# A hybrid encoder block on one core: when raw weight tiles are loaded and summed, and where the sine tables stand

## The chip, the cores and the metric

The kernel runs on one core of one Trainium2 chip. The time is device microseconds of one execution; of several executions the median is given. The core has five engines that run their own instruction streams: the matmul engine (PE), two that work on vectors (DVE and ACT), POOL, and SP, which here only issues DMAs. Each engine takes its instructions in the order in which they were put into its stream; between engines they wait for each other by semaphores.

## The reference

One layer on 512 tokens of width 1024, in float32: a SwiGLU FFN (inner width 2816) at half weight, a mixer of gated DeltaNet heads beside multi-head latent attention, and a second FFN. Each part reads a modulated norm of the stream.

```
mod = sc @ w_ada[l] + b_ada[l]
sh1, s1, g1, sh2, s2, g2, sh3, s3, g3 = jnp.split(mod, N_MOD, axis=-1)
h = _modulate(x, sh1, s1)
x = x + 0.5 * g1[:, None, :] * _swiglu(h, ffn1_w_in[l], ffn1_w_out[l])
h = _modulate(x, sh2, s2)
y = _hybrid_mixer(h, cos, sin, w_in[l], ...)
x = x + g2[:, None, :] * y
h = _modulate(x, sh3, s3)
x = x + 0.5 * g3[:, None, :] * _swiglu(h, ffn2_w_in[l], ffn2_w_out[l])
```

`cos` and `sin` are taken of the positions times 32 frequencies; the attention's rotary keys and queries use them. `mod` is the product of the 1024 conditioning values with a 1024 x 9216 matrix.

## The kernel before

**Products in three parts.** Every float32 product runs as three matmuls (`mm3`, lines 278 to 282, and 906 to 908 for the pairs): a high part of the weight (`wh`, a rounded copy made by ACT) and of the activation, and the low parts that are left (`wl`, the difference, made by DVE). A raw weight tile (`wr`, 512 KB, four buffers) is loaded by SP, copied to its high part by ACT, and subtracted to its low part by DVE.

**FFN1** (`ffn1`, `ffn_pairs`) runs as a hand-written order: one counter of steps, and for every step a list of tasks (`add(step, task)`); `tick` runs the tasks of a step, then come the step's matmuls, then `side.step`. Within `in_order` every engine keeps the order in which the instructions are written. Steps 0 to 47 are the units of inner columns 6 to 11 (8 steps each, `whole` and `piece`); their SwiGLU activation is `glu_steps`, at the end of the unit. From step 48 (`begin`) ten pairs follow, one for each of the inner column blocks 12 to 21, 7 steps apart (`base` = 48, 55, ..., 111; `stop` = 111). Beside them the down projection is fed at 1 to 1.33 products a step (`down`, whose weights are loaded 8 steps ahead of their use, `add(s - 8)`).

**A pair** (`pair_tasks`, `product`) is one gate column block and one up column block, computed with seven products of half width instead of eight. It takes two raw tiles, `g` and `u`. Its tasks, as steps from its base: `load` (-11, both tiles, on SP); `sums` (-7, lines 802 and 803, DVE: `sx` and `sy` from `g` and `u`), `sums2` (-5, DVE); the high part of `u` (-6, line 825, ACT); its low part, which here is not a subtraction on DVE: ACT writes the negated high tile (-5, line 836) and an accumulating DMA on POOL's queue adds the raw tile to it (`add_low`, -4, line 843); high and low parts of `x` (-4, -3) and `y` (-3, -2); of the second half of `g` (0, 1). Then, while PE runs the products `up0` (0), `up1` (1), `s2` (3), `s3` (4), `s1` (6), `s4` (9), `gate1` (12), the accumulator is copied between them by ACT (`early_copy`, line 849: `cc` at 1, `uc` at 4, `cc` again at 7), and the activation is put together: `both` (8), `gate1` (9), `act1` (11), `gate0` (13, lines 858 and 859), `act0` (15, lines 868 and 870: the product `cc` and its high part `ah`), `act_low` (16, line 874: `al`). `s2` adds to the accumulator that `early_copy` at 1 reads, so PE's `s2` waits for that copy.

**The side work** (`Side`, `side.step(n)`: resume a generator n times) holds first the modulation sums (`ada`): 112 tiles of `w_ada`, each loaded by POOL's queue (line 579) and added with a scale on DVE (line 590), one a resumption. It takes 121 resumptions, 81 of them done by step 48. Behind it stands `mixer_consts`: its first resumption issues the loads of the small vectors (`cw`, `vb`, positions) on SP, the fifth transposes `cw` on PE (line 1187) and copies `cwT` and the positions on DVE (lines 1189, 1191), the sixth transposes the positions (line 1194) and forms the angles; then come the sine and cosine by range reduction and polynomials (`sincos`, lines 1269 to 1307) and the rotary tables (lines 1217, 1219): 53 DVE operations. In the pairs' stage `side.step` runs in 3 of 7 steps for the first three pairs and 5 of 7 after, one resumption each; from step 111, two a step.

**Behind the pairs** (steps 111 to 123 and `close`) the last 6 blocks of the down projection run (`units`: high part line 1052, low part line 1056), while the last pair is finished. Then the norm of the mixer follows in two halves (lines 454 to 482), and `latents`: the first projections (three units with both halves of the tokens), a fourth, and so on; `gather` splits them. `mixer` then runs dense units of four parts each with side chains beside them (`dense_units`, `Rates`); the rotary tables are first read in `prep_q`. Outside `in_order` the instructions of an engine can be put into another order than that of the program.

Of the kernel before, what the change touches and what calls it, by code (L numbers as in the profile page):

```python
# [18 lines left out]
P = 128  # L19
# [70 lines left out]
class Block:  # L90
# [687 lines left out]
        yield  # L778
        v.tensor_tensor(out=fl, in0=t, in1=fh.bitcast(F32), op=ALU.subtract)

    def pair_tasks(self, w, f, base, add, room=None, side=None):


        nc, v = self.nc, self.nc.vector
        r = {}
        late = 1 if side else 0
        flat = lambda t: t.rearrange("p k f -> p (k f)")
        A, B = slice(0, NT), slice(NT, 2 * NT)

# [38 lines left out]
        def lo(name, src, part=slice(0, 2 * NT)):  # L828
            def go():
                if name == "g1" and room:  # L830
                    for i in range(2):
                        v.tensor_tensor(out=r["g1l"][i], in0=r[src][:, part.start + i * HALF:part.start + i * HALF + HALF],
                                        in1=r["g1h"][i].bitcast(F32), op=ALU.subtract)
                    return
                if name == "u" and side:
                    nc.scalar.activation(r["ul"], r["u"], AF.Copy, scale=-1.0)
                    return
                v.tensor_tensor(out=r[name + "l"], in0=r[src][:, part], in1=r[name + "h"].bitcast(F32), op=ALU.subtract)
            return go

        def add_low():
            if side:
                nc.gpsimd.dma_start(r["ul"].bitcast(F32), r["u"], accum_op=ALU.add)

        def early_copy(name, part):
            def go():
# [30 lines left out]
        r["do"] = dict(load=load, sums=sums, sums2=sums2)  # L877
        for n, src, part in (("u", "u", slice(0, 2 * NT)), ("x", "x", slice(0, 2 * NT)), ("y", "y", slice(0, 2 * NT)), ("g1", "g", B)):
            r["do"][n] = hi(n, src, part), lo(n, src, part)
        for i, (at, go) in enumerate(((-11, load), (-7, sums), (-5, sums2), (-6, hi("u", "u")), (-5 if side else -4, lo("u", "u")), (-4, hi("x", "x")),  # L880
                       (-3, lo("x", "x")), (-3, hi("y", "y")), (-2, lo("y", "y")), (-1 + late, hi("g1", "g", B)),
                       (0 + late, lo("g1", "g", B)), (1, early_copy("cc", L)), (4, early_copy("uc", L)), (7, early_copy("cc", H)),
                       (8, both), (9, gate1), (11, act1), (13, gate0), (15, act0), (16, act_low), (-4, add_low))):
            by_hand = 11 if base == 0 else 1 if base == 7 else 0
            if i >= by_hand:
                add(base + at, go)
# [47 lines left out]
    def ffn_pairs(self, w1, w2, gate, plain, raws, split, accs, side=None):  # L934
# [7 lines left out]
        begin = 8 * len(grid)  # L942
        base = [begin + 7 * j for j in range(n)]
        stop = base[-1]
        pairs = [self.pair_tasks(w1, plain + j, base[j], add, (2 * (j % 2), 2 * (j % 2) + 1) if side else None, side)
                 for j in range(n)]

        def whole(g, f):

            def load(i):  # L950
                raws[i] = self.raw_unit(w1, i)

            for e in range(2):
                i, s, r = 2 * f + e, 8 * g + 4 * e, {}
                add(s - 9, lambda i=i: load(i))
                add(s - 4, lambda i=i, r=r: next(r.setdefault("g", self.unit_split(raws, split, i))))
                add(s - 3, lambda r=r: next(r["g"], None))
            r = {}
            add(8 * g + 8, lambda: next(r.setdefault("g", self.glu_steps(accs, f))))
            add(8 * g + 9, lambda: next(r["g"], None))  # L960

        def piece(g, f, o):
            i, k = 2 * f + o // 4, 2 * (o % 4)
# [106 lines left out]
        for s in range(0, stop + 13):  # L1070
            if s == begin - 7 and side:
                self.early_pool.__exit__(None, None, None)
                sums = self.tc.tile_pool(name="ws", bufs=1)
                self.ws = sums.__enter__()
            tick(s)
            if s < begin:
                piece(s // 8, grid[s // 8], s % 8)
            for j in range(n):
                if s - base[j] in STEPS:
                    self.product(pairs[j], STEPS[s - base[j]])  # L1080
            for go in fill.pop(s, []):
                go()
            if s in last:
                steps_of(*last[s])
            if side:
                at = s - begin
                side.step(1 + (s % 4 == 0) if at < 0 else at % 7 in ((1, 3, 6) if at < 21 else (0, 1, 3, 4, 6)) if s < stop else 2)
        assert not fill
        if side:
            sums.__exit__(None, None, None)  # L1090
# [73 lines left out]
    def mixer_consts(self):  # L1164
        nc, ins = self.nc, self.ins
        cw = self.slot(s="cw")[:57, :P]
        pos_i = self.slot(I32, s="posi")[:NB, :P]
        vb = self.const([P, 136], s="vb")
        with self.tc.issue_after(self.loaded.ins):
            self.load(cw[:48, :], ins["gdn_conv_w"][0].rearrange("j (t p) -> (j t) p", p=P))  # L1170
            self.load(pos_i, ins["positions"].rearrange("o (b p) -> (o b) p", p=P))
            row = 48
            self.vcol = {}
            for name, n in (("mla_q_norm_w", 3), ("mla_kv_norm_w", 2), ("gdn_norm_w", 1), ("qkn_q_nope", 1),
                            ("qkn_k_nope", 1), ("mla_out_norm_w", 1)):
                self.load(cw[row:row + n, :], ins[name].rearrange("o (t p) -> (o t) p", p=P))
                self.vcol[name] = row
                row += n
            o = 0
            for name, n in (("gdn_a_log", 4), ("gdn_dt_bias", 4), ("qkn_q_rope", 64), ("qkn_k_rope", 64)):  # L1180
                self.load(vb[:, o:o + n], ins[name][0].partition_broadcast(P))
                o += n
        self.alog, self.dtb, self.gqr, self.gkr = vb[:, 0:4], vb[:, 4:8], vb[:, 8:72], vb[:, 72:136]
        for _ in range(4):
            yield
        p = self.aux()
        nc.tensor.transpose(p[:, :57], cw, self.ident[:57, :57])
        self.cwT = self.const([P, 57], s="cwT")
        nc.vector.tensor_copy(self.cwT, p[:, :57])
        pos_f = self.slot(s="posf")[:NB, :P]  # L1190
        nc.vector.tensor_copy(pos_f, pos_i)
        yield
        p = self.aux()
        nc.tensor.transpose(p[:, :NB], pos_f, self.ident[:NB, :NB])
        pos = self.const([P, NB], s="pos")
        nc.vector.tensor_copy(pos, p[:, :NB])


        fr = self.slot(s="fr")[:, :32]
        for i in range(32):  # L1200
            nc.gpsimd.memset(fr[:, i:i + 1], float(np.float32(10000.0 ** (-i / 32.0))))
        ang = self.slot(s="ang")[:, :P]
        av = ang.rearrange("p (b i) -> p b i", b=NB)
        nc.vector.tensor_tensor(out=av, in0=self.bc(pos, NB, 32), in1=fr.unsqueeze(1).to_broadcast([P, NB, 32]),
                                op=ALU.mult)
        yield
        cos, sin = yield from self.sincos(ang)
        yield
        cv, sv = cos.rearrange("p (b i) -> p b i", b=NB), sin.rearrange("p (b i) -> p b i", b=NB)
        self.rope_c, self.rope_s = {}, {}  # L1210
        for nm, gain, sc in (("q", self.gqr, 192.0 ** -0.5), ("k", self.gkr, 1.0)):
            both = self.slot(s="rope").rearrange("p (e b c) -> p e b c", e=2, b=NB)
            c, s = both[:, 0], both[:, 1]
            for j in range(2):
                gj = gain[:, 32 * j:32 * j + 32].unsqueeze(1).to_broadcast([P, NB, 32])
                go = gain[:, 32 - 32 * j:64 - 32 * j].unsqueeze(1).to_broadcast([P, NB, 32])
                nc.vector.scalar_tensor_tensor(out=c[:, :, 32 * j:32 * j + 32], in0=cv, scalar=sc, in1=gj, op0=ALU.mult,
                                               op1=ALU.mult)
                nc.vector.scalar_tensor_tensor(out=s[:, :, 32 * j:32 * j + 32], in0=sv, scalar=sc if j else -sc, in1=go,
                                               op0=ALU.mult, op1=ALU.mult)  # L1220
                yield
            self.rope_c[nm], self.rope_s[nm] = c, s
        self.gqn = self.const([P, 1], s="gqn")
        j = self.vcol["qkn_q_nope"]
        nc.vector.tensor_scalar(out=self.gqn, in0=self.cwT[:, j:j + 1], scalar1=192.0 ** -0.5, scalar2=None, op0=ALU.mult)

    def masks(self):
        nc = self.nc
# [101 lines left out]
    def latents(self, nb):  # L1330
# [8 lines left out]
        def gather(ps):  # L1339
# [8 lines left out]
                    nc.vector.tensor_tensor(out=acc, in0=acc, in1=sq, op=ALU.add)  # L1348
            return parts, acc

        pk = self.proj(self.aux())
        qp, acc = gather(ps)
        ps = [pk]
        lq = qp, self.rms_cols(self.colsum(acc), NB, 384)
        p = self.proj()
# [1 line left out]
        nc.scalar.copy(s[:72, :], p[:72, :])  # L1357
        wq = next(wq)
        ps.append(self.proj())
        kp, acc = gather(ps)  # L1360
        lkv = kp, self.rms_cols(self.colsum(acc), NB, 256)
        wkv = next(wkv)
# [690 lines left out]
    def mixer(self, nb):  # L2053
# [39 lines left out]

        att.add(prepared())

        self.dense_units(4, Rates(sides, (1, 0, 0.25)), 1, conv_done(4, kT))
        chain.flush()
        silu(kT)

# [145 lines left out]
```

## Time and profile before

| what | us |
|---|---|
| median of 3 executions | 1052.04 (1050.21 to 1052.23) |
| the profiled execution | 1052.18 |
| its span, first to last instruction | 1050.2 |
| PE busy in the span | 1022.4 |
| DVE busy | 755.4 |
| ACT busy | 483.2 |

The granted clock of PE is 0.999 of full speed over the span. In the rows of the profile, a line such as "0.9 <-ACT ah L870" behind the last bar says that the engine sat idle for 0.9 us until ACT's instruction of line 870, which writes `ah`, was done. Rows of the timeline give the start, the duration, engine, line, operation, output and inputs, and in brackets the idle time ahead and who ended it. The time of a PE row overlaps with the next one, since matmuls are pipelined: the distance between starts is what one costs. The stretches' rows give, for PE, weight loads, DVE, ACT and POOL, the busy time and the number of instructions.

### The profile page before, as it was taken

The page shows a single profiled execution, that of the slowest core. Times are in us where ns is not written, and L with a number is a line of the kernel's source. Part 1 is how long each engine was busy: PE and PEld are TensorE (multiplying, and loading weights), DVE is VectorE, ACT ScalarE, POOL GpSimd, SP SyncE. Part 2 cuts the span into 40 slices and gives each one's busy share as a digit, 9 for nine tenths or more (in the row PEclk, how much of TensorE's full clock was granted, in tenths as well). Part 3 has the DMA queues.
Part 4 walks back from the last instruction along what each step waited for, and adds up shares of the span by engine and source line. Part 5 has one row for each costly group of instructions (what it writes and reads, how often), then busy time and mean ns, then how long its engine had stood idle before and what let it go on. Part 6 is the DMA issues. An engine that isn't in the chain of part 4 may idle for free. (4 is left out here: it accounts for less than half of the span.)

```text
span 1050.2 us, 17055 instructions
## 1 busy us (share of the span) xinstructions
PE 1022.4 (97%) x6655; PEld 888.4 (85%) x6655; DVE 755.4 (72%) x1414; ACT 483.2 (46%) x864; POOL 114.6 (11%) x232
## 2 busy tenths in 40 slices
PE   7999999999999999999999999999999999999998
PEld 5787878879888979888877768898999999999987
DVE  4477998787788687547976756689768778777642
ACT  4342232255354336649566563465345444444431
POOL 0033331222120101000001011210000000000000
PEclk9999999999999999999999999999999999999999
DMA  9997886676775337611311201073423333333222
GB/s 273 289 272 230 286 245 196 204 193 188 213 200 156 95 96 198 160 41 42 90 51 36 71 22 55 28 161 101 135 78 103 108 101 111 94 98 104 77 61 81
DMA packets 187278, 140.21 MB, mean 134 GB/s; under 512 B 14385, under 2 KB 176190, under 8 KB 187198
## 3 DMA queue, kind: packets, MB, share of 16 engines
q1 hardware_dynamic: 175646, 100.33, 33.4%
q0 software_dynamic: 11552, 38.81, 13.5%
q8 instruction: 52, 0.85, 0.3%
q14 instruction: 28, 0.23, 0.1%
HBM read 127.18 MB, written 2.49 MB: 123 GB/s over the span
## 5 line engine op out<-in xcount | busy, mean ns | idle before, releaser
L280 PE MATMUL pa<-ah,wh 128*128 128x512 f32 (+1 forms) x346 | 133.1, 385 | 1.3 <-ACT ah L870 0.9
L281 PE MATMUL pa<-al,wh 128*128 128x512 f32 (+1 forms) x346 | 132.7, 384 | 1.5 <-DVE al L874 1.5
L282 PE MATMUL pa<-ah,wl 128*128 128x512 f32 (+1 forms) x346 | 131.0, 379 | 0.0
L281 PE MATMUL pa<-hl,wh 128*128 128x512 f32 (+1 forms) x293 | 109.4, 373 | 1.6 <-DVE hl L474 1.4
L280 PE MATMUL pa<-hh,wh 128*128 128x512 f32 (+1 forms) x293 | 110.2, 376 | 0.4 <-ACT hh L482 0.4
L282 PE MATMUL pa<-hh,wl 128*128 128x512 f32 (+1 forms) x293 | 108.5, 370 | 0.0
L579 POOL DMA_DIRECT2D ar<-in_w_ada x112 | 62.9, 606 | 170.1 <-DVE aa L590 63.7
L982 DVE SCALAR_TENSOR_TENSOR xT<-pa,mod,xT 128x512 f32<-128x512 f32 (+1 forms) x79 | 57.3, 728 | 33.1 <-PE pa L282 33.0
L282 PEld LDWEIGHTS pa<-ah,wl 128*128 128x128 f32 x346 | 65.2, 188 | 13.0 <-DVE wl L1056 0.2
L590 DVE SCALAR_TENSOR_TENSOR aa<-ar,sc,aa 128x512 f32<-128x512 f32 x98 | 73.3, 748 | 1.3
L280 PEld LDWEIGHTS pa<-ah,wh 128*128 128x128 f32 x346 | 65.9, 190 | 7.8 <-ACT ah L870 1.3
L281 PEld LDWEIGHTS pa<-al,wh 128*128 128x128 f32 x346 | 65.9, 190 | 7.4 <-DVE al L874 2.2
L906 PE MATMUL pb<-fh,wh 128*128 128x256 f32 x224 | 63.9, 285 | 3.4 <-ACT cc L849 3.3
L280 PEld LDWEIGHTS pa<-hh,wh 128*128 128x128 f32 x293 | 55.3, 189 | 12.4 <-issue 2.9
L281 PEld LDWEIGHTS pa<-hl,wh 128*128 128x128 f32 x293 | 55.3, 189 | 10.5 <-DVE hl L474 2.6
L908 PE MATMUL pb<-hh,wl 128*128 128x256 f32 x224 | 63.4, 283 | 0.7 <-DMA wl<-wr 0.7
L208 DVE TENSOR_TENSOR wl<-wr,wh 128x1024 fp32r<-128x1024 f32 (+1 forms) x33 | 38.5, 1166 | 35.6 <-ACT wh L203 35.4
L282 PEld LDWEIGHTS pa<-hh,wl 128*128 128x128 f32 x293 | 55.3, 189 | 10.3 <-issue 1.2
L908 PE MATMUL pb<-fh,wl 128*128 128x256 f32 x224 | 63.3, 283 | 0.0
L907 PE MATMUL pb<-fl,wh 128*128 128x256 f32 x224 | 63.3, 283 | 0.0
L907 PE MATMUL pb<-hl,wh 128*128 128x256 f32 x224 | 63.3, 282 | 0.0
L906 PE MATMUL pb<-hh,wh 128*128 128x256 f32 x224 | 63.2, 282 | 0.0
(448 smaller groups left out, 2786.9 us busy)
## 6 DMA issues: line engine op xcount, KB each, us to landing
wr<-in_ffn_w_in SPq DMA_DIRECT2D x82, 512.0 KB, 4.0
ar<-in_w_ada POOLq DMA_DIRECT2D x112, 256.0 KB, 4.7
wr<-in_ffn_w_out SPq DMA_DIRECT2D x32, 512.0 KB, 4.0
wr<-in_w_in SPq DMA_DIRECT2D x21, 512.0 KB, 4.1
wl<-wr POOLq DMA_DIRECT2D x18, 512.0 KB, 5.9
ar<-in_w_ada SPq DMA_DIRECT2D x16, 512.0 KB, 8.2
wr<-in_ffn_w_out SPq DMA_DIRECT2D x16, 384.0 KB, 3.6
wr<-in_w_out SPq DMA_DIRECT2D x8, 512.0 KB, 3.4
```

Source lines behind the costliest of these rows:

```text
L208: self.nc.vector.tensor_tensor(out=lo, in0=raw, in1=hi.bitcast(F32), op=ALU.subtract)
L280: mm(out, wh, xh, start=start, stop=False)
L281: mm(out, wh, xl, start=False, stop=False)
L282: mm(out, wl, xh, start=False, stop=stop)
L579: nc.gpsimd.dma_start(tiles[i], a1[kc * P:(kc + 1) * P, o:o + NT])
L590: nc.vector.scalar_tensor_tensor(out=acc, in0=a, scalar=sc, in1=acc, op0=ALU.mult, op1=ALU.add)
L906: mm(out, wh, xh, start=start and k == 0, stop=False, **kw)
L907: mm(out, wh, xl, start=False, stop=False, **kw)
L908: mm(out, wl, xh, start=False, stop=stop and k == 3, **kw)
L982: nc.vector.scalar_tensor_tensor(out=self.xT[t][:, ts], in0=p[:, ts], scalar=gate()[:, t:t + 1], in1=self.xT[t][:, ts], op0=ALU.mult, op1= ...
```

## The change

It has four parts, all in the order of work; no instruction is added to or taken from the computation.

1. In FFN1's pairs, `load` moves from -11 to -9, `sums` from -7 to -5, `sums2` from -5 to -3, the parts of `x` from -4 and -3 to -2 and -1, those of `y` from -3 and -2 to -1 and 0. The parts of `u`, the accumulating DMA and the parts of `g` keep their steps. For the first pair, `load` stays at -11 and the parts of `u` and the accumulating DMA come two steps earlier (`early`). FFN2's pairs keep their steps.
2. `glu_steps` is put at the front of its step instead of behind the tasks that are there.
3. The modulation sums run as 1, 0, 0, 2, 0, 1, 0 resumptions in the seven steps of every pair.
4. `mixer_consts` ends with the angles; the sine and rotary tables become `sine_tables`, a side chain of their own, resumed 4, 1 and 2 times in `latents` and once for each part of the mixer's first dense units.

```
-    def pair_tasks(self, w, f, base, add, room=None, side=None):
+    def pair_tasks(self, w, f, base, add, room=None, side=None, early=False):
...
-        for i, (at, go) in enumerate(((-11, load), (-7, sums), (-5, sums2), (-6, hi("u", "u")), (-5 if side else -4, lo("u", "u")), (-4, hi("x", "x")),
-                       (-3, lo("x", "x")), (-3, hi("y", "y")), (-2, lo("y", "y")), (-1 + late, hi("g1", "g", B)),
-                       (0 + late, lo("g1", "g", B)), (1, early_copy("cc", L)), (4, early_copy("uc", L)), (7, early_copy("cc", H)),
-                       (8, both), (9, gate1), (11, act1), (13, gate0), (15, act0), (16, act_low), (-4, add_low))):
+        ahead = 2 if early else 0
+        if side:
+            before = ((-9 - ahead, load), (-6 - ahead, hi("u", "u")), (-5 - ahead, lo("u", "u")), (-4 - ahead, add_low),
+                      (-5, sums), (-3, sums2), (-2, hi("x", "x")), (-1, lo("x", "x")), (-1, hi("y", "y")),
+                      (0, lo("y", "y")), (0, hi("g1", "g", B)), (1, lo("g1", "g", B)))
...
+        for i, (at, go) in enumerate((*before, (1, early_copy("cc", L)), (4, early_copy("uc", L)), (7, early_copy("cc", H)),
+                       (8, both), (9, gate1), (11, act1), (13, gate0), (15, act0), (16, act_low))):
...
-            add(8 * g + 8, lambda: next(r.setdefault("g", self.glu_steps(accs, f))))
-            add(8 * g + 9, lambda: next(r["g"], None))
+            tasks.setdefault(8 * g + 8, []).insert(0, lambda: next(r.setdefault("g", self.glu_steps(accs, f))))
+            tasks.setdefault(8 * g + 9, []).insert(0, lambda: next(r["g"], None))
...
-                at = s - begin
-                side.step(1 + (s % 4 == 0) if at < 0 else at % 7 in ((1, 3, 6) if at < 21 else (0, 1, 3, 4, 6)) if s < stop else 2)
+                side.step(1 + (s % 4 == 0) if s < begin else (1, 0, 0, 2, 0, 1, 0)[(s - begin) % 7] if s < stop else 2)
...
+        self.tables = Side()
+        self.tables.add(self.sine_tables(ang))
+
+    def sine_tables(self, ang):
+
+        nc = self.nc
         cos, sin = yield from self.sincos(ang)
-        yield
...
+        self.tables.step(4)
         pk = self.proj(self.aux())
         qp, acc = gather(ps)
+        self.tables.step(1)
...
+        self.tables.step(2)
         kp, acc = gather(ps)
...
-        self.dense_units(4, Rates(sides, (1, 0, 0.25)), 1, conv_done(4, kT))
+        self.dense_units(4, Rates((*sides, self.tables), (1, 0, 0.25, 1)), 1, conv_done(4, kT))
+        self.tables.flush()
```

More of the change, by code (lines that the diff above doesn't have):

```diff
@@ L779, in token_sums @@
         v.tensor_tensor(out=fl, in0=t, in1=fh.bitcast(F32), op=ALU.subtract)
-    def pair_tasks(self, w, f, base, add, room=None, side=None):
+    def pair_tasks(self, w, f, base, add, room=None, side=None, early=False):
         nc, v = self.nc, self.nc.vector
         r = {}
-        late = 1 if side else 0
         flat = lambda t: t.rearrange("p k f -> p (k f)")
@@ L841, in add_low @@
         def add_low():
-            if side:
-                nc.gpsimd.dma_start(r["ul"].bitcast(F32), r["u"], accum_op=ALU.add)
+            nc.gpsimd.dma_start(r["ul"].bitcast(F32), r["u"], accum_op=ALU.add)
         def early_copy(name, part):
@@ L879, in pair_tasks @@
             r["do"][n] = hi(n, src, part), lo(n, src, part)
-        for i, (at, go) in enumerate(((-11, load), (-7, sums), (-5, sums2), (-6, hi("u", "u")), (-5 if side else -4, lo("u", "u")), (-4, hi("x", "x")),
-                       (-3, lo("x", "x")), (-3, hi("y", "y")), (-2, lo("y", "y")), (-1 + late, hi("g1", "g", B)),
-                       (0 + late, lo("g1", "g", B)), (1, early_copy("cc", L)), (4, early_copy("uc", L)), (7, early_copy("cc", H)),
-                       (8, both), (9, gate1), (11, act1), (13, gate0), (15, act0), (16, act_low), (-4, add_low))):
+        ahead = 2 if early else 0
[3 more added lines that the diff above has]
+                      (0, lo("y", "y")), (0, hi("g1", "g", B)), (1, lo("g1", "g", B)))
+        else:
+            before = ((-11, load), (-7, sums), (-5, sums2), (-6, hi("u", "u")), (-4, lo("u", "u")), (-4, hi("x", "x")),
+                      (-3, lo("x", "x")), (-3, hi("y", "y")), (-2, lo("y", "y")), (-1, hi("g1", "g", B)),
+                      (0, lo("g1", "g", B)))
+        for i, (at, go) in enumerate((*before, (1, early_copy("cc", L)), (4, early_copy("uc", L)), (7, early_copy("cc", H)),
+                       (8, both), (9, gate1), (11, act1), (13, gate0), (15, act0), (16, act_low))):
             by_hand = 11 if base == 0 else 1 if base == 7 else 0
@@ L944, in ffn_pairs @@
         stop = base[-1]
-        pairs = [self.pair_tasks(w1, plain + j, base[j], add, (2 * (j % 2), 2 * (j % 2) + 1) if side else None, side)
+        pairs = [self.pair_tasks(w1, plain + j, base[j], add, (2 * (j % 2), 2 * (j % 2) + 1) if side else None, side, j == 0)
                  for j in range(n)]
@@ L1205, in mixer_consts @@
                                 op=ALU.mult)
-        yield
+        self.gqn = self.const([P, 1], s="gqn")
+        j = self.vcol["qkn_q_nope"]
+        nc.vector.tensor_scalar(out=self.gqn, in0=self.cwT[:, j:j + 1], scalar1=192.0 ** -0.5, scalar2=None, op0=ALU.mult)
+        self.tables = Side()
+        self.tables.add(self.sine_tables(ang))
+    def sine_tables(self, ang):
+        nc = self.nc
         cos, sin = yield from self.sincos(ang)
-        yield
         cv, sv = cos.rearrange("p (b i) -> p b i", b=NB), sin.rearrange("p (b i) -> p b i", b=NB)
@@ L1222, in mixer_consts @@
             self.rope_c[nm], self.rope_s[nm] = c, s
-        self.gqn = self.const([P, 1], s="gqn")
-        j = self.vcol["qkn_q_nope"]
-        nc.vector.tensor_scalar(out=self.gqn, in0=self.cwT[:, j:j + 1], scalar1=192.0 ** -0.5, scalar2=None, op0=ALU.mult)
     def masks(self):
```

## The prediction

> **What bounds the kernel now.** I read the page first, then the busy time of two stretches, then the timeline engine by engine.
>
> ```profile
> span 1050.2 us, 17055 instructions
> PE 1022.4 (97%) x6655; PEld 888.4 (85%) x6655; DVE 755.4 (72%) x1414; ACT 483.2 (46%) x864; POOL 114.6 (11%) x232
> ...
> L281 PE MATMUL pa<-al,wh 128*128 128x512 f32 (+1 forms) x346 | 132.7, 384 | 1.5 <-DVE al L874 1.5
> ...
> L906 PE MATMUL pb<-fh,wh 128*128 128x256 f32 x224 | 63.9, 285 | 3.4 <-ACT cc L849 3.3
> ```
>
> The matmul queue (PE) is the bound: it has work in 1022.4 of 1050.2 us, so a change that leaves the matmuls alone can only win what PE waits. The groups show the waits in reach, behind the last bar: 3.3 us for the copy `cc` (L849), 1.5 for `al` (L874). Next, where they lie (PE's busy time is the second number behind the stretch):
>
> ```profile
> 204.00:345.00 141.00, 136.96 (x937) 123.85 (x936) 114.56 (x178) 68.59 (x114) 24.93 (x69) 1.00 0.68 181
> 345.00:383.00 38.00, 35.61 (x219) 30.75 (x218) 29.09 (x89) 10.83 (x21) 3.58 (x13) 1.00 0.30 81
> ...
> 412.00:450.00 38.00, 38.00 (x228) 34.32 (x227) 23.41 (x41) 22.88 (x38) 3.88 (x4) 1.00 0.58 149
> ```
>
> 204 to 345 is the stage of the pairs (steps 48 to 110), 345 to 383 what follows. PE idles 141.00 - 136.96 = 4.04 us in the first: `cc` 3.3, and 0.7 for a DMA into `wl` that the next rows show. In the second it idles 38.00 - 35.61 = 2.39: `al` 1.5 and `ah` 0.9 (rows further down). A wait costs a little more than the idle time shown:
>
> ```profile
> 219.37 0.28 PE L906 MATMUL pb<-hh,wh 128*128 128x256 f32 x1
> 219.49 0.28 PE L907 MATMUL pb<-hl,wh 128*128 128x256 f32 x1
> 220.48 0.38 PE L908 MATMUL pb<-hh,wl 128*128 128x256 f32 x1 [0.72 <-DMA wl<-wr]
> 220.70 0.28 PE L906 MATMUL pb<-hh,wh 128*128 128x256 f32 x1
> ```
>
> Unhindered, such matmuls start 0.12 us apart (219.37, 219.49). From 219.49 to 220.48 are 0.99 us and to 220.70 another 0.22: 0.97 us lost for 0.72 shown, so **0.25 us more per wait**.
>
> **Why PE waits for `cc`.** One pair, its engines in order of time:
>
> ```profile
> 276.20 0.89 POOL L843 DMA_DIRECT2D wl<-wr  x1 [2.94 <-ACT wl L836]
> ...
> 281.87 0.37 SPq L128 DMA_DIRECT2D wr<-in_ffn_w_in  x1
> ...
> 286.68 0.69 DVE L803 TENSOR_TENSOR sx<-wr,wr 128x512 f32<-128x512 f32 x1 [3.48 <-DMA wr<-in_ffn_w_in]
> ...
> 289.60 0.62 ACT L870 CAST ah<-cc 128x512 fp32r<-128x512 f32 x1 [6.06 <-DVE cc L868]
> 290.12 0.36 ACT L849 COPY cc<-pb 128x256 f32<-128x256 f32 x1
> 290.38 1.05 ACT L825 CAST wh<-wr 128x1024 fp32r<-128x1024 f32 x1
> ...
> 291.65 1.05 ACT L836 ACTIVATE wl<-wr 128x1024 fp32r<-128x1024 f32 x1
> ...
> DVE sx L803 <- DMA wr<-in_ffn_w_in: 21.8, 8, 3.9
> ...
> SPq L128 <- DMA wl<-wr: 116.4, 18, 23.7
> ```
>
> DVE reaches `sums` (L803) of the next pair before its raw tile `u` has landed and stands (3.48 us here, 21.8 us over 8 pairs). Behind it stands L868 of an older pair; ACT's L870 waits for that (6.06); behind L870 stands L849, the copy that frees the accumulator; PE's `s2` waits for L849. It is also a loop. SP, which issues the loads, waits 18 times for an accumulating DMA (last row, of the waits of SP's queue): the one of 276.20 frees the buffer that the next `u` is loaded into (issued 281.87, 5.67 us later); it lands when L803 starts (286.68, 4.81 later); ACT reaches `u`'s high part only at 290.38 (3.70), and the next accumulating DMA can go at 292.70 (2.32, end of L836). A turn is 16.5 us. PE's own work for 7 steps is 84 x 0.12 = 10.1 plus, where the down projection runs one product a step, 21 matmuls at 0.23 (382.21 and 382.44 below) = 4.8: 14.9 us. The loop is slower than PE, and PE pays.
>
> **The change part by part.**
>
> *Sums and x, y parts two steps later.* No instruction is added. `sums` of pair j now stands at step +2 of pair j-1, behind L868 (+1) and the `cc` copy (+1), where it stood at +0. SP does not wait for steps: it issues a load when its buffer is free, as 281.87 shows, so what "load two steps later" changes is only its place in SP's queue, and that not: from pair 1 loads move from 44, 51, 58, ... to 46, 53, 60, ..., and no down load (46, 54, 62, 70, 78, 84, 90, 96) is passed, the pair's coming first at 46. So `u` lands as before or sooner, while its first DVE reader comes some 4.5 us later (a step is (345-204)/63 = 2.24 us), more than the longest wait, 3.9. The loop loses the 3.70 us: 12.8 us, below PE's 14.9. ACT's high half of `u` stays at -6 and is the first to meet `u`; it stands behind the `cc` copy of its step, so a wait there no longer holds PE's `s2`, only `uc` (+4, needed at +6). Later `x` and `y` parts are ready at -1 and 0, used from +3 and +6: 3 steps, 6.7 us, cover their parts of about 1 us (L825: 1.05). Gone: 3.3 and 0.25 for each of the four waits (near 212, 274, 290 and 307 us), **4.3 us** (bounds 0 and 4.3).
>
> The Trainium skill, DMA: Bandwidth & Descriptors, section Rules for kernel authors, says to issue a DMA early, compute, and wait for it late. By it a load issued two steps later lands two steps later, the waits stay, and this part is worth 0; the issue of 281.87, ruled by a buffer, does not bear that out.
>
> *First pair two steps earlier, glu first in its step.* Both move `u` of pair 0 and 1 through ACT sooner; the 0.97 us at 220.48 (pair 1's accumulating DMA) needs one step. Bounds 0 and 1.0; I take half, **0.5**, since POOL's queue before that DMA is unchanged.
>
> *Modulation sums 1, 0, 0, 2, 0, 1, 0 a pair.* 36 resumptions instead of 39 by step 111, the last four in the two steps after it. DVE is busy 114.56 of 141 us there and isn't the bound, and the last modulation is first used in the second FFN. 0, with the 3 of 39 too small to bound.
>
> *Sine tables away from steps 111 to 123.*
>
> ```profile
> 359.14 0.23 DVE L1269 COPY sr<-ang 128x128 f32<-128x128 f32 x1
> ...
> 378.11 0.15 DVE L1225 TENSOR_SCALAR gqn<-cwT 128x1 f32<-128x1 f32 x1
> 378.18 0.41 DVE L858 TENSOR_TENSOR uc<-uc,pb 128x256 f32<-128x256 f32 x1
> ...
> 379.83 0.62 ACT L870 CAST ah<-cc 128x512 fp32r<-128x512 f32 x1
> ...
> 374.52 0.28 PE L908 MATMUL pb<-fh,hl 128*128 128x256 f32 x1
> ...
> 380.50 0.51 PE L280 MATMUL pa<-ah,wh 128*128 128x512 f32 x1 [0.91 <-ACT ah L870]
> 381.41 0.50 PE L281 MATMUL pa<-al,wh 128*128 128x512 f32 x1 [0.41 <-DVE al L874]
> ...
> 382.21 0.39 PE L281 MATMUL pa<-al,wh 128*128 128x512 f32 x1
> 382.44 0.40 PE L282 MATMUL pa<-ah,wl 128*128 128x512 f32 x1
> ...
> 372.63 0.50 PE L281 MATMUL pa<-al,wh 128*128 128x512 f32 x1 [1.07 <-DVE al L874]
> ```
>
> The 53 table operations, from the first row to the second, hold DVE for 19.1 us, some 14 of them their own: between them stand eight operations of the pairs of 0.4 to 1 us. The last pair's product ends at 374.80, yet its L858 starts at 378.18, behind the tables: 3.4 us late. From L858 to `ah` are 379.83 + 0.62 - 378.18 = 2.3 us; started at 374.9 it ends at 377.2, before PE asks (379.6). Gone: 0.91 + 0.41 + 1.07 idle and 3 x 0.25, **3.1 us** (bounds 1.5, if half the tables still run there, and 3.1).
>
> *The tables in the latents.* Four pieces go ahead of the fourth projection, three later, thirteen into the 16 parts of the first dense units.
>
> ```profile
> 411.67 0.49 DVE L480 SCALAR_TENSOR_TENSOR hm<-xT,mod,rb 128x256 f32<-128x256 f32 x1 [1.35 <-ACT rb L464]
> ...
> 423.90 1.23 DVE L208 TENSOR_TENSOR wl<-wr,wh 128x1024 fp32r<-128x1024 f32 x1 [5.53 <-ACT wh L203]
> ...
> 464.67 1.23 DVE L208 TENSOR_TENSOR wl<-wr,wh 128x1024 fp32r<-128x1024 f32 x1 [7.59 <-ACT wh L203]
> ```
>
> DVE's idle 5.53 us before 423.90 holds the first four pieces (13 operations, at 19.1 / 53 = 0.36 us at most 4.7); the 7.59 us before 464.67 and gaps like it hold the others. Cost 0 (upper bound 12.7, second rival).
>
> *The constants.* With the modulation ending two steps later, their DMAs move from step 111 to 113, behind one more down load in SP's queue, and both transposes now come in one step with nothing between:
>
> ```profile
> 345.77 0.48 SPq L128 DMA_DIRECT2D cw<-in_gdn_conv_w  x1
> ...
> 349.11 0.36 SPq L128 DMA_DIRECT2D vb<-in_gdn_a_log  x1
> ...
> 354.44 14.44 SPq L128 DMA_DIRECT2D wr<-in_ffn_w_out  x5
> ...
> 356.48 0.27 PE L1187 MATMUL pb<-ident,cw 57*128 57x57 f32 x1
> 358.29 0.22 PE L1194 MATMUL pb<-ident,posf 4*128 4x4 f32 x1
> ...
> 356.78 0.22 DVE L1189 COPY cwT<-pb 128x57 f32<-128x57 f32 x1 [0.89 <-PE pb L1187]
> ```
>
> Today a product lies between L1187 and L1194 and hides DVE's two copies (L1189's 0.22 and another like it, L1191). Side by side, PE would stand from the end of L1187's 0.19 us slot for both copies and the hand-overs, 356.67 to about 357.3, and 0.1 to restart: **+0.7 us**. The DMAs go behind the load of 354.44: all of `cw` within 3.3 us (345.77 to 349.11), and 2.5 to land (349.11 to 351.62, L1454's row below): 360.6 at the latest. PE arrives at 358.44, the end of L1194's slot, plus the products of steps 114 and 115 (12 at 0.12, 6 at 0.23): 361.3. Bounds 0.5, and 4 if they miss it by 3 us.
>
> *Sum* against the profiled execution, 1052.18 us (span 1050.2 and 2.0 around it; 0.14 above the median of 1052.04): 1052.18 - 4.3 - 0.5 - 3.1 + 0.7 = **1045.0**. From 412 to 450 PE has no gap (38.00 of 38.00), so what is won ahead of it isn't waited away there.
>
> **The rivals.** *The wait goes along with the sums.* If `u` lands later by as much as its reader moved, or ACT stands for it instead and `uc` comes late, only the tail is won: 1052.2 - 3.1 + 0.7 = 1049.8. For it: all 8 waits for `u` are there today, and ACT, one queue, meets `u` first then; against: the issue at 281.87, free of steps, and a loop shorter than PE's work. The Trainium skill's rule above would have this case.
>
> *Slower: tables ahead of the second half's norm.* Instructions need not run where they stand in the program:
>
> ```profile
> 351.62 0.17 DVE L1454 COPY ex<-vb 128x4 f32<-128x4 f32 x1 [3.67 <-DMA vb<-in_gdn_a_log]
> ```
>
> L1454 belongs to the gates of the mixer, yet ran here, and held DVE 3.67 us. If the tables run as one block ahead of L480 at 411.67, their 14 us meet 1.35 us of idle, and PE, for which the half is normed, loses up to 12.7: 1058. It turns the sum at 7.2 + 1.35 = 8.6 us of table work there. Against: DVE's long gaps lie behind.
>
> *Late constants.* PE waits 4 us at L1187: 1048.3. For: SP's queue; against: 1 us of margin.
>
> **How the numbers follow.** Forecast 0.60, wait goes along 0.17, late constants 0.13, tables ahead 0.10. A measurement of this kernel tells some 0.2% (2.1 us) from no change. Faster: 0.58 + 0.10 + half of 0.17 = 0.76; within: 0.14; slower 0.10. The forecast's own range is 1042.5 (all bounds good, the mixer behind falling a little better) to 1047.5; with the first and third rival 1042 to 1051.5.
>
> **What would show it.** Right: L803's wait falls from 21.8 to under 5 us, the `cc` wait of L906 from 3.3 to under 1, no wait for `ah` or `al` near 380, tables after 412, PE idle in the two stretches from 6.4 to about 1.5. Wrong: ACT's L825 waiting for `wr`, PE waiting at L1187 for over 1 us, or table lines ahead of L480.

## The result, and the profile after

| what | before | after |
|---|---|---|
| median of the runs, us | 1051.64 (4 runs, 1050.21 to 1052.23) | 1045.45 (4 runs, 1043.34 to 1046.85) |
| the profiled execution, us | 1052.18 | 1044.66 |
| its span, us | 1050.2 | 1042.9 |

The ratio is 0.9941, with a 95% interval of 0.992 to 0.9963: 6.2 us faster, between 3.9 and 8.4. In the page of the kernel after, the row of busy shares and three groups of PE answer to those shown of before:

```profile
PE 1021.5 (98%) x6655; PEld 890.2 (85%) x6655; DVE 756.0 (72%) x1414; ACT 483.7 (46%) x864; POOL 115.8 (11%) x232
...
L280 PE MATMUL pa<-ah,wh 128*128 128x512 f32 (+1 forms) x346 | 132.8, 384 | 0.1
L281 PE MATMUL pa<-al,wh 128*128 128x512 f32 (+1 forms) x346 | 132.4, 383 | 0.0
...
L911 PE MATMUL pb<-fh,wh 128*128 128x256 f32 x224 | 63.4, 283 | 0.5 <-ACT cc L847 0.5
```

The waits for `ah` and `al` are gone. Of the 3.3 us for `cc` (L911 is L906 of before, L847 its L849) 0.5 is left. PE's busy time has hardly moved, so the gain is time in which PE stood. By groups (line, engine, operation, tiles and shapes, count; busy time, mean ns of one; idle time ahead and who ended it), the stretch of the pairs, 204 to 345 us, of the kernel after:

```profile
L911 PE MATMUL pb<-fh,wh 128*128 128x256 f32 x72 | 20.5, 284 | 0.5 <-ACT cc L847 0.5
...
L824 ACT CAST wh<-wr 128x1024 fp32r<-128x1024 f32 x9 | 9.5, 1053 | 5.5 <-DMA wr<-in_ffn_w_in 3.7 <-ACT cc L847 1.7
...
L802 DVE TENSOR_TENSOR sx<-wr,wr 128x512 f32<-128x512 f32 x9 | 6.2, 684 | 0.0
```

L802 is the sum in front of which DVE stood 21.8 us (L803 of before). DVE now stands for nothing there. ACT stands for the raw tile in its place (L824, 3.7 us), as the first reader, and nobody on the path waits for that. On the timeline of PE, four matmuls of the kernel after show what is left and what is new:

```profile
210.91 0.38 PE L911 MATMUL pb<-fh,wh 128*128 128x256 f32 x1 [0.46 <-ACT cc L847]
...
355.32 0.27 PE L1191 MATMUL pb<-ident,cw 57*128 57x57 f32 x1
356.01 0.22 PE L1198 MATMUL pb<-ident,posf 4*128 4x4 f32 x1 [0.43 <-DVE posf L1195]
...
424.57 0.61 PE L552 MATMUL pb<-ones,lsq 128*128 128x1 f32 x4 [1.05 <-DVE lsq L1356]
```

The second and third are the two constant transposes, now side by side. The last wait is new and was not foreseen: in the latents, the column sums wait for squares that DVE adds up late. DVE's timeline says why:

```profile
408.53 0.22 DVE L1277 COPY sr<-ang 128x128 f32<-128x128 f32 x1
...
416.26 0.23 DVE L1292 TENSOR_SCALAR sr<-sr 128x128 f32<-128x128 f32 x1
416.44 1.23 DVE L208 TENSOR_TENSOR wl<-wr,wh 128x1024 fp32r<-128x1024 f32 x1
417.58 0.68 DVE L1324 TENSOR_TENSOR latl<-pa,lath 128x512 fp32r<-128x512 f32 x1
```

From 408.53 to 416.44 stand 26 table operations in a block (and one L474), 7.9 us; before, the gap there was 5.53 us.

**Where the 7.3 us of the span come from.** The same matmul, read in both timelines, shows how far the kernel after is ahead. What PE loses at a wait is the time from the start of the matmul ahead of it to the start of the one that waited, less the usual distance of two starts.

| stretch (by the kernel before) | ahead by | what of it |
|---|---|---|
| up to 205 us | 0.5 | nothing of the change: start-up |
| 205 to 312 | 5.3 | 4.8 more: `cc` 3.7, the accumulating DMA 1.0 |
| 312 to 405 | 9.0 | 3.7 more: `ah`, `al` 3.0, two waits in their wake 0.6, small ones; less 0.8 for the transposes |
| to the column sums at 433 | 7.8 | 1.2 given back |
| to 677 | 7.9 | |
| to 684 | 6.5 | 1.4 given back: half clock, below |
| to the end | 7.3 | the last output, 0.8 |

In a few stretches the granted clock of PE is 0.50; matmuls that otherwise start 0.12 us apart then start 0.21 us apart (in the kernel after at 671.20 and 671.41 us). Such a stretch is called half clock here. The one of the kernel after stands behind two waits that both kernels have, of the same length in both. First the timeline of PE after, then that of before:

```profile
668.79 0.66 PE L1842 MATMUL pb<-ident,on 128*128 128x128 f32 x4 [1.18 <-DVE on L1328]
670.22 0.39 PE L280 MATMUL pa<-mh,wh 128*128 128x256 f32 x1 [0.77 <-ACT mh L1850]
```

```profile
676.66 0.66 PE L1831 MATMUL pb<-ident,on 128*128 128x128 f32 x4 [1.18 <-DVE on L1320]
678.09 0.38 PE L280 MATMUL pa<-mh,wh 128*128 128x256 f32 x1 [0.77 <-ACT mh L1839]
```

In the windows of the kernel after (stretch; length, busy time and instructions of PE, weight loads, DVE, ACT, POOL; granted clock; DMA share; GB/s), the clock is halved for one stretch behind them:

```profile
667.08:670.49 3.41, 1.46 (x10) 0.94 (x8) 2.08 (x7) 1.11 (x5) 1.45 (x2) 1.00 0.00 0
670.49:673.90 3.41, 3.41 (x16) 3.29 (x16) 1.50 (x6) 0.51 (x3) 0.00 (x0) 0.50 0.00 0
```

In those of before it is not:

```profile
673.32:676.73 3.41, 2.23 (x20) 2.03 (x19) 1.57 (x3) 1.10 (x3) 1.59 (x3) 1.00 0.00 0
676.73:680.14 3.41, 2.63 (x18) 2.20 (x19) 2.02 (x8) 1.11 (x4) 0.60 (x1) 1.00 0.00 0
```

So 1.4 us of this one comparison of profiles are half clock behind waits that the change did not touch. Over all executions the two kernels are not alike in this. One such stretch, 3.41 of some 1043 us, takes the granted clock of the whole span to 0.998. On record at 0.998 or lower are 8 of the 9 executions of the changed kernel (four here, five below) and 17 of 34 of the kernel before. How much of this is the change's own doing no run separates; one part, behind the new wait of the column sums, shows below.

### The profile page after: what moved, and what is told of

Same layout as the page of the kernel before. It is cut to its first block, busy times and chain, and to the rows that moved or that the text cites. A ratio compares the mean times of both kernels' runs of the same rounds, so it can differ in the third digit from the quotient of the medians.

```text
span 1042.9 us, 17049 instructions
## 1 busy us (share of the span) xinstructions
PE 1021.5 (98%) x6655; PEld 890.2 (85%) x6655; DVE 756.0 (72%) x1414; ACT 483.7 (46%) x864; POOL 115.8 (11%) x232
## 5 line engine op out<-in xcount | busy, mean ns | idle before, releaser
L282 PEld LDWEIGHTS pa<-ah,wl 128*128 128x128 f32 x346 | 65.1, 188 | 12.8
L911 PE MATMUL pb<-fh,wh 128*128 128x256 f32 x224 | 63.4, 283 | 0.5 <-ACT cc L847 0.5
L911 PE MATMUL pb<-hh,wh 128*128 128x256 f32 x224 | 63.1, 282 | 0.0
L280 PE MATMUL pb<-hh,wh 128*128 128x512 f32 x149 | 58.6, 393 | 0.0
```

What stands on the lines that cost most here:

```text
L280: mm(out, wh, xh, start=start, stop=False)
L282: mm(out, wl, xh, start=False, stop=stop)
L911: mm(out, wh, xh, start=start and k == 0, stop=False, **kw)
```

## The experiments

The runs of the kernel before beside them had medians of 1051.52 us (18 runs, with the first four), 1051.45 (7, the next four) and 1051.25 (9, the last two). Ratios are to these. Where a difference is under 2 us it is read from waits, not from times.

**The pairs alone.** The kernel before, with `pair_tasks` of the changed kernel and the first pair's lead:

```diff
-                       (-11, load), (-7, sums), (-5, sums2), ...
+            before = ((-9 - ahead, load), (-6 - ahead, hi("u", "u")), ...
+                      (-5, sums), (-3, sums2), (-2, hi("x", "x")), ...
```

> Nothing is left out: the kernel before with the pairs' new steps alone (loads, sums, x and y parts, first pair's lead); sine tables, modulation rates and the order of the gating are those of before. Theory (the sums stood on DVE for a raw tile and held up the cc copies): the 21.8 us that DVE waits for raw tiles in front of the sums go to under 1, PE's waits for cc fall from 3.3 to under 1, the wait for the accumulating DMA near 220 us goes; 4 to 5 us under the kernel before, 1046.5 to 1047.5; the waits for ah and al near 380 us (2.4 idle) stay. Rival (most of the gain comes from the tables): 1049 or more.

1046.23 us (4 runs), ratio 0.9953 (0.9938 to 0.9967): 5 us faster. By groups, from 190 to 470 us:

```profile
L280 PE MATMUL pa<-ah,wh 128*128 128x512 f32 (+1 forms) x122 | 45.8, 375 | 1.1 <-ACT ah L868 0.9 <-DVE xT L987 0.2
L281 PE MATMUL pa<-al,wh 128*128 128x512 f32 (+1 forms) x122 | 45.7, 375 | 1.5 <-DVE al L872 1.5
...
L911 PE MATMUL pb<-fh,wh 128*128 128x256 f32 x80 | 22.7, 284 | 0.0
L913 PE MATMUL pb<-hh,wl 128*128 128x256 f32 x80 | 22.7, 284 | 0.4 <-DMA wl<-wr 0.4
...
L802 DVE TENSOR_TENSOR sx<-wr,wr 128x512 f32<-128x512 f32 x10 | 6.8, 682 | 0.0
```

The `cc` waits are all gone, more than in the whole change, where 0.5 is left; `ah` and `al` still wait, as they must. Against the theory, 0.4 us of the wait for the accumulating DMA is still there, although the first pair has its lead.

**The tables alone.** The changed kernel, with `pair_tasks`, the modulation rates and the order of the gating of the kernel before, so that this is left of the diff:

```diff
+        self.tables = Side()
+        self.tables.add(self.sine_tables(ang))
+
+    def sine_tables(self, ang):
...
         cos, sin = yield from self.sincos(ang)
...
+        self.tables.step(4)
...
```

> Nothing is left out: the changed kernel with the pairs' steps, modulation rates and gating order of the kernel before, so that the sine tables alone are moved. Theory: the waits for ah and al near 380 us go (2.4 us idle, 3.1 with the restarts), 1.2 comes back as a wait of the column sums for the squares in the latents, because four pieces of the tables stand on DVE ahead of its first split; the cc waits (3.3) stay; 1.5 to 2.5 us under the kernel before, about 1049.7. Rival (the tables in the latents cost nothing and the new wait there has another cause): 3 us under, no wait of the column sums.

1048.33 us (9 runs), ratio 0.997 (0.9956 to 0.9984): 3 us faster (1.7 to 4.6), where the theory had 1.5 to 2.5. By groups, 190 to 470 us:

```profile
L281 PE MATMUL pa<-al,wh 128*128 128x512 f32 (+1 forms) x122 | 45.5, 373 | 0.0
...
L906 PE MATMUL pb<-fh,wh 128*128 128x256 f32 x80 | 23.2, 290 | 2.5 <-ACT cc L849 2.5
...
L803 DVE TENSOR_TENSOR sx<-wr,wr 128x512 f32<-128x512 f32 x9 | 6.2, 692 | 19.2 <-DMA wr<-in_ffn_w_in 19.1
...
L552 PE MATMUL pb<-ones,lsq 128*128 128x1 f32 x16 | 2.0, 246 | 1.0 <-DVE lsq L1352 1.0
```

The sums stand for their raw tiles and `cc` waits, as before; the new wait of the column sums (L552) is there without any change to the pairs. It belongs to the tables. By the medians the two parts win 5.3 and 3.2 us, 8.5 together, and the whole change 6.2. Of the difference, 0.7 at the `cc` copy near 211 us and 0.8 at the transposes are in neither part (both are tried below); the rest is within the intervals.

**The sums back at their steps, the rest as changed.**

```diff
-                      (-5, sums), (-3, sums2), (-2, hi("x", "x")), ...
+                      (-7, sums), (-5, sums2), (-2, hi("x", "x")), ...
```

> Nothing is left out: the changed kernel with the two parts of the sums put back two steps (to the steps of the kernel before), everything else as changed. Theory: DVE waits for raw tiles in front of the sums again (10 to 22 us in all, from under 1), and PE's waits for cc come back from 0.5 to 2 to 3.3 us; 2 to 4.5 us over the changed kernel, 1047.5 to 1050. Rival (it is the later x and y parts, or the rates, that freed the cc copies): within 1 us of the changed kernel, PE's cc waits under 1 us.

1051.16 us (10 runs), ratio 0.9996 (0.9987 to 1.0006): all that the change wins is lost again, 5.7 us, more than the theory's 4.5. By groups, then the longest wait on PE's timeline, then windows:

```profile
L911 PE MATMUL pb<-fh,wh 128*128 128x256 f32 x80 | 23.5, 294 | 5.0 <-ACT cc L847 5.0
...
L802 DVE TENSOR_TENSOR sx<-wr,wr 128x512 f32<-128x512 f32 x10 | 6.9, 689 | 14.0 <-DMA wr<-in_ffn_w_in 14.0
```

```profile
291.40 0.39 PE L911 MATMUL pb<-fh,wh 128*128 128x256 f32 x1 [2.31 <-ACT cc L847]
```

```profile
288.24:291.65 3.41, 1.10 (x7) 0.62 (x6) 3.41 (x7) 1.19 (x3) 0.00 (x0) 1.00 0.33 98
291.65:295.06 3.41, 3.41 (x15) 3.21 (x15) 3.34 (x6) 2.79 (x5) 1.21 (x3) 0.50 0.68 210
673.95:677.36 3.41, 1.47 (x11) 1.02 (x10) 1.81 (x5) 1.11 (x4) 1.45 (x2) 1.00 0.00 0
677.36:680.77 3.41, 3.40 (x15) 3.31 (x16) 1.55 (x7) 0.77 (x3) 0.00 (x0) 0.50 0.00 0
```

One line of the program, the sums' places alone, brings back DVE's wait and PE's. In the profiled execution the 2.31 us for `cc` were also followed by a stretch of half clock, which costs up to 3.41 / 2 = 1.7 us more; a second one lies near 677 us.

**The first pair without its lead.**

```diff
-... if side else None, side, j == 0)
+... if side else None, side)
```

> Nothing is left out: the changed kernel without the first pair's lead of two steps for u's high part, low part and accumulating DMA. Theory: 0.5 to 1 us of PE's waits come back near 210 to 222 us (for cc or for the accumulating DMA); 0.5 to 1 over the changed kernel, within what its time can tell, so it is read from the waits. Rival (the gating first in its step took that wait away): no wait there, no difference.

1044.94 us (4 runs), ratio 0.9938 (0.9922 to 0.9955): no difference from the changed kernel. The groups:

```profile
L911 PE MATMUL pb<-fh,wh 128*128 128x256 f32 x80 | 22.7, 284 | 0.5 <-ACT cc L847 0.5
L913 PE MATMUL pb<-hh,wl 128*128 128x256 f32 x80 | 22.6, 282 | 0.0
```

There is no wait for the accumulating DMA. The theory falls: the lead does nothing that the profile shows. With the lead and the gating behind its step's other tasks (the pairs alone) 0.4 us stayed. With the gating first it is 0 without the lead, as here, and with it, also at the modulation rates that the pairs alone had (the modulation sums as before, below). So it is the gating that takes away the 0.4.

**No tables in the latents.**

```diff
-        self.tables.step(4)
         pk = self.proj(self.aux())
         qp, acc = gather(ps)
-        self.tables.step(1)
...
-        self.tables.step(2)
```

> Nothing is left out: the changed kernel without the seven pieces of the sine tables in the latents, so that all of them go into the first dense units of the second half. Theory (the four pieces ahead of the first split hold DVE some 8 us, 1.5 more than PE leaves it): PE's wait of the column sums for the squares near 424 us (1.05 idle, 1.2 with the restart) goes; 1.2 under the changed kernel, about 1044.2, less what the tables then delay in the dense units. Rival (the wait there belongs to the latents' own chain of splits): it stays, no gain.

1043.87 us (4 runs), ratio 0.9922 (0.9908 to 0.9937). By DVE's timeline and by groups:

```profile
408.89 0.49 DVE L474 SCALAR_TENSOR_TENSOR hl<-hm,mod,hh 128x256 fp32r<-128x256 f32 x1 [0.18 <-ACT hh L482]
414.84 1.23 DVE L208 TENSOR_TENSOR wl<-wr,wh 128x1024 fp32r<-128x1024 f32 x1 [5.47 <-ACT wh L203]
```

```profile
L552 PE MATMUL pb<-ones,lsq 128*128 128x1 f32 x16 | 1.9, 240 | 0.0
```

DVE's gap is back, L208 starts 1.6 us earlier than after (414.84 against 416.44, with PE level to 0.1), and the wait is gone, as the theory said. The tables' operations run between 439 and 478 us then.

**The tables behind the first gathering.** The three calls become one, `self.tables.step(7)`, at the place of the third.

> Nothing is left out: the changed kernel with the seven pieces of the sine tables in one place, behind the first gathering and its column sums and ahead of the second gathering. Theory: the wait near 424 us goes (1.2), but the second gathering's column sums, some 13 us later, may wait instead: between 1.2 under the changed kernel and 1 over it. Rival: no difference at 424 us.

1045.74 us (4 runs), ratio 0.9947 (0.9927 to 0.9967): nothing won. The wait at 424 us is gone, and another stands further on, on PE's timeline:

```profile
443.66 0.44 PE L280 MATMUL pa<-uh,lath 128*128 128x384 f32 x1 [1.73 <-ACT upo L1428]
```

It isn't the second gathering's column sums, as expected, but ACT's copy behind them, which empties an accumulator. There the tables stand between DVE's splits (`latl`, L1324), and ACT, which waits for these (2.41 us for one of them), comes late.

**The transposes apart.** A second `yield` ahead of the transpose of the positions.

> Nothing is left out: the changed kernel with the transpose of the positions one step behind that of the constants, where they stand side by side now. Theory: PE's wait for the copied positions near 356 us (0.43 idle, 0.8 with the restart) goes and nothing takes its place; 0.7 under the changed kernel, read from the waits, since its time can't tell that. Rival (PE stands there for something else too): the wait moves to the next product.

1044.61 us (4 runs), ratio 0.9933 (0.9917 to 0.9949). The transpose's group, from 190 to 470 us (its line is one further down):

```profile
L1199 PE MATMUL pb<-ident,posf 4*128 4x4 f32 x1 | 0.2, 220 | 0.0
```

Its 0.43 us of idle are gone, and no other wait of PE there takes their place.

**The modulation sums as before.**

```diff
-                side.step(1 + (s % 4 == 0) if s < begin else (1, 0, 0, 2, 0, 1, 0)[(s - begin) % 7] if s < stop else 2)
+                at = s - begin
+                side.step(1 + (s % 4 == 0) if at < 0 else at % 7 in ((1, 3, 6) if at < 21 else (0, 1, 3, 4, 6)) if s < stop else 2)
```

> Nothing is left out: the changed kernel with the modulation sums spread over the steps as in the kernel before (three to five steps a pair with one each). Theory of the prediction (the new spread is worth 0 in the pairs): PE's waits between 204 and 345 us as in the changed kernel, where 0.46 idle for cc is left at 211 us; the constants come earlier and their transposes apart, so 0.7 less near 356 us. Rival (the sums on DVE in those steps are what is left of the cc wait): that wait goes or grows by over 0.3 us.

1043.99 us (4 runs), ratio 0.9926 (0.9911 to 0.9941). ACT's timeline ahead of `s2` of the first pair, here and, in the next fence, in the changed kernel:

```profile
209.64 0.37 ACT L847 COPY cc<-pb 128x256 f32<-128x256 f32 x1 [0.55 <-PE pb L912]
```

```profile
210.48 0.37 ACT L847 COPY cc<-pb 128x256 f32<-128x256 f32 x1 [2.35 <-PE pa L282]
```

The rival holds, though not by its mechanism: the 0.46 us for `cc` go, and with them the transposes' wait. The copy does not wait for a sum on DVE. It reads `pb`, and yet its releaser is a product of the down projection into `pa`, which reads `ah`. In the program `cc`, `ah`, `al` and a modulation sum's tile `aa` all take their buffers from one pool (`slot`, 56 buffers). DVE's timeline shows that the wait moves from one of them to another, first in the changed kernel, then here:

```profile
207.92 0.48 DVE L588 TENSOR_SCALAR aa<-ar,sc 128x512 f32<-128x512 f32 x1
210.33 0.69 DVE L707 TENSOR_TENSOR al<-af,ah 128x512 fp32r<-128x512 f32 x1 [1.93 <-PE pa L281]
```

```profile
211.22 0.49 DVE L588 TENSOR_SCALAR aa<-ar,sc 128x512 f32<-128x512 f32 x1 [0.98 <-PE pa L281]
```

In the changed kernel a new `aa` (L588) starts ahead of `al` and `cc` and without a wait, and these two wait for products that still read an older `al` and `ah`. Here `al` and `cc` come first and do not wait for one, and `aa` does. That fits buffers of one pool that are handed on in the order in which they are asked for; no run gave `cc` a buffer of its own, so the reading is not tested.

**Both together, and the changed kernel once more.** The modulation sums as before and no tables in the latents; beside it the changed kernel, unchanged.

> Nothing is left out: the changed kernel with the modulation sums spread as in the kernel before and with all pieces of the sine tables in the first dense units. Theory (the two gains are of different waits and add): no wait of PE for cc near 211 us, none for the positions near 356, none of the column sums near 424; 0.6, 0.8 and 1.2 with their restarts, 2.5 us under the changed kernel: about 1043. Rival (they take each other's place in the latents or the dense units): 1044 to 1045.

> Nothing is left out: the changed kernel once more, beside the one above. Theory: the same waits; whether 3.4 us at half clock stand behind the waits near 670 us depends on where these fall, not on the kernel, so they may be missing here; 1044 to 1046.5. Rival (the half clock is of this kernel): 1.4 to 1.7 us lost at the same place again.

The first: 1042.93 us (5 runs, 1040.58 to 1042.97), ratio 0.9908 (0.989 to 0.9926), the lowest of all and under the changed kernel's 1045.62 (5 runs), ratio 0.9936 (0.992 to 0.9952). The gains add, 2.7 us by the medians, where 2.5 were expected; the intervals of the two ratios just overlap, so the size is carried by the waits. Two of the five executions, 1040.58 and 1041.24 us, have a granted clock of 1.000, and the other three, 1042.93 to 1042.97, one of 0.998: half clock comes and goes with the same program. By groups from 190 to 470 us of the first:

```profile
L911 PE MATMUL pb<-fh,wh 128*128 128x256 f32 x80 | 22.7, 284 | 0.0
...
L552 PE MATMUL pb<-ones,lsq 128*128 128x1 f32 x16 | 1.9, 240 | 0.0
...
L1199 PE MATMUL pb<-ident,posf 4*128 4x4 f32 x1 | 0.2, 219 | 0.0
```

The changed kernel's second profile has the same waits as its first, and two stretches of half clock where the first had one:

```profile
423.41:426.82 3.41, 2.37 (x15) 1.82 (x14) 1.69 (x3) 0.42 (x1) 0.49 (x1) 1.00 1.08 291
426.82:430.23 3.41, 3.41 (x10) 2.62 (x9) 0.61 (x1) 1.69 (x3) 0.54 (x1) 0.50 0.93 230
669.18:672.59 3.41, 1.46 (x9) 0.82 (x8) 2.32 (x8) 1.23 (x4) 1.43 (x2) 1.00 0.00 0
672.59:676.00 3.41, 3.41 (x17) 3.41 (x18) 1.26 (x5) 0.64 (x2) 0.00 (x0) 0.50 0.00 0
```

The one near 427 us was not in the first profile of the same program, so it does not come in every execution. But the wait in the stretch ahead of it is that of the column sums (1.04 us), which the tables in the latents brought; in the profile of the tables alone half clock follows the same wait, from 430.96 us on. So this wait costs 1.2 us, and in some executions up to 1.7 us more. The one near 672 came again, as the rival had it. It does not come in every execution either: one of the changed kernel's first four, of 1043.34 us, has a granted clock of 1.000.

## Why the prediction was right, and where it was not

1045.0 us were forecast and 1045.45 measured; the forecast case is the one that happened. Its terms, one by one, against what PE lost in the two profiles:

| step | forecast | measured | shown by |
|---|---|---|---|
| sums and x, y parts later | 4.3 won | 4.4 won | the sums back, the pairs alone |
| first pair's lead, gating first | 0.5 won | 1.0 won, and as much without the lead | the lead taken away |
| modulation sums 1, 0, 0, 2, 0, 1, 0 | 0 | 0.7 lost: the `cc` wait left at 211 us, so that 3.7 of the 4.4 remain | the modulation sums as before |
| tables out of the tail | 3.1 won | 3.0 won, and 0.6 in their wake | the tables alone |
| tables in the latents | 0 | 1.2 lost | no tables in the latents |
| two transposes side by side | 0.7 lost | 0.8 lost | the transposes apart |

*The sums.* The chain was right link by link: the raw tile, DVE's sums, the operation behind them, `ah`, the copy, PE. Moving the two sums back brings all of it back, with nothing else touched. That moving the load does nothing by itself fits the traces: in SP's queue the weight loads of the pairs' stage stand in the same order in both kernels, and in the kernel with the sums back, whose loads keep their later step, the load that was issued at 281.87 us before is issued at 281.94. The load alone was not moved in any run. The forecast that ACT would be the first to meet `u` at no cost holds: 3.7 us of waiting, none of it PE's.

*The loop.* A turn without the wait was put at 12.8 us, and PE's own at 14.9. From the accumulating DMA of one pair to that of the next are now 14.9, 16.2 and 14.7 us (on POOL's timeline, issued at 270.67, 285.61, 301.83 and 316.52), 15.3 on the mean, where a turn took 16.5. With the sums back it is 16.2 again (issued at 244.92, 260.46, 276.40, 293.85 and 309.58). The 14.9 holds for one product of the down projection a step, and some steps have more, so 15.3 is near PE's own pace; its waits say the same.

*The step that failed* is "DVE's idle 5.53 us before 423.90 holds the first four pieces (13 operations, ... at most 4.7)". The program does put 13 operations ahead of the split, and 26 ran there: those of the pieces behind the first gathering and of the next units came forward in the instruction order; in the program each reads only `ang` or what table operations ahead of it wrote. The 26 hold DVE 7.9 us. That instructions need not run where they stand in the program was the premise of the second rival, which looked for it ahead of the norm and priced it at up to 12.7 us. It happened one stage later, for 1.2. With it fell the prediction's remark that what is won ahead of 412 us isn't waited away up to 450 us: that held for the kernel before, in which no tables stood there.

*The modulation rates* were costed at nothing, because DVE is not the bound. DVE is not, but with the new rates ACT's copy stands for a product on PE, and PE for the copy. That the two are bound by a buffer of the shared pool is what the traces fit, not what a run tried.

*The rivals.* That the wait goes along with the sums (1049.8) is out: L802 waits 0.0 us. The Trainium skill's rule that spoke for it (DMA: Bandwidth & Descriptors, Rules for kernel authors: issue early, wait late) is not against this change when read to its end; what the change moved is the wait, which came later, while the load still issues when its buffer is free. Late constants: L1191 has no wait in the timeline, as forecast. Tables ahead of the norm: the first table operation, at 408.53, stands behind all of the norm but one L474.

*What the prediction could not have had* is the half clock of 1.4 us in one profile and not in the other. That the forecast lies within 0.5 us of the measured median is partly luck: 0.7 and 1.2 us that were missed stand against 0.5 and 0.6 won beyond the forecast, and half clock falls on some executions and not on others.

## What to carry to other kernels

Where an engine with an in-order queue stands for a load, look at what is queued behind the waiting instruction, and move the reader, not the load: an instruction whose data may be late belongs behind the copies that free an accumulator. Work that is moved into another engine's gap has to be counted as it will run, not as it stands in the program: independent operations come forward and fill more of the gap than was meant. Side work that costs its engine nothing can still take a buffer of a shared pool ahead of an operation on the path: here, as far as the traces show, it did.

## What the runs showed of the hardware

Two waits of 1.18 and 0.77 us, less than 1.5 us apart, cost PE about 2.3 us in some executions and up to 1.7 more in others, in which the granted clock then is 0.50 for 3.41 us. In the 12 profiles here it followed these two waits seven times. The stretches lie on a grid: in the profile with the sums moved back they begin at 291.65 and 677.36, and 385.71 us between them are 113 times 3.413. Laying that grid over each profile, through the stretches that it has (the last one, behind PE's final matmul, is in all), gives the idle time of PE that fell into one cell of the grid. Where all 1.95 us did (the changed kernel twice, the sums back, to 0.01, and no lead), the next cell ran at half clock each time. Where the waits were split over two cells, 1.18 and 0.77 (before, both together) or 0.92 and 1.03 (the pairs alone), it never did. Between these, 1.48, 1.59 and 1.61 were followed by half clock, and 1.65 and 1.67 were not. The windows of the last of these, the kernel with the tables behind the first gathering:

```profile
667.57:670.98 3.41, 1.74 (x14) 1.30 (x12) 1.71 (x5) 0.91 (x3) 1.52 (x3) 1.00 0.00 0
670.98:674.39 3.41, 3.13 (x23) 2.93 (x24) 2.05 (x8) 1.47 (x5) 0.00 (x0) 1.00 0.00 0
```

There were 14 matmuls in the cell, where the changed kernel had 10 and 9. Three other stretches, at 399.00 us (no lead), 426.82 (the changed kernel again) and 430.96 (the tables alone), followed cells with only 1.01 to 1.04 us idle, and 1.54 us in the cell that ends at 568.09 us in the changed kernel was followed by full clock. So idle time alone is not the rule, and what else enters is open.

The Trainium skill (TensorE: Matmul & The Clock Gate, Part 1) states a free-running window of 3413 ns, which the runs here bear out: 113 times 3.413 us between two stretches of one run. The advice on the same page of the Trainium skill in "Why this matters for your kernels", no idle gaps over some 3 us, is too generous for this kernel: no gap near 670 us is over 1.2 us.
